# Out-projection: one burst of fp32 work per tile, with TensorE in written order

## The chip, the cores and the metric

The kernel runs on one core of a Trainium2 chip. The core has five engines that run side by side, each with its own queue in order: TensorE (PE in the profile; its weight loads are the row PEld), VectorE (DVE), ScalarE (ACT), GpSimd (POOL) and SyncE (SP, which only issues DMAs here). TensorE writes to PSUM, eight banks of 512 fp32 columns on 128 partitions; VectorE and ScalarE read PSUM. The metric is the time of one execution on the device in microseconds, as a median of several runs.

## The reference

One layer of a diffusion backbone on 256 context tokens and 2048 latent tokens, 18 tiles of 128 tokens in all. Tiles 0 and 1 are the context, 2 to 17 the latent tokens.

```python
h = rms_norm(x, g_pre) * (1 + scale) + shift
u = h @ w_in
z, xbc, dt_raw, ga, gb, gsil = split(u)
y_ssd, h_fin = ssd_branch(z, xbc, dt_raw, ..., h0)        # two scans over chunks of 128 tokens, forward and backward
    # y = y_f + y_b + d_skip * xs;  y = y * silu(z);  y = rms_norm(y, norm_g)
y_conf = conformer_branch(ga, gb, ...)                    # gate, depthwise conv, layer_norm, silu
y_conf = y_conf * silu(gsil)
out = concatenate([y_ssd, y_conf], -1) @ w_out            # 2048 -> 1024 channels
return x + gate * rms_norm(out, g_post), h_fin
```

## The kernel before

Everything up to the out-projection (input projection, convolutions, forward scan, Conformer convolution) leaves its results in DRAM. The out-projection then takes one tile of 128 tokens after the other, in `order`: 17 down to 2, then 1 and 0, since the backward scan carries its state from late tiles to early ones. `a` counts the tiles, `i` is the tile at hand, `nxt` the next one.

For each tile TensorE does 96 large matmuls (L1069, `out_part`): 16 blocks k of 128 input channels, each as three products (high x high, high x low, low x high parts, fp32r) for two halves of 512 output columns. Blocks 0 to 7 read the SSD half of the input (`yh`, `yl`), blocks 8 to 15 the Conformer half (`ph`, `pl`). The sums of a tile grow in two PSUM banks, `pso[i]`.

Between them lie smaller fp32 instructions, which prepare later tiles:

- `ssd_pre(i)`: the carried state `Sb` times C (L976, `qo`, 8 matmuls, 16 instructions in the profile), added to the stored y (L977, L978), times z (L979), squared on ScalarE (L980) and summed to `zr` (L982); then POOL carries `Sb` on (L988, L989). Its inputs ct, el, y, z and st come by DMA.
- `ssd_norm(i)`: the sum of squares over partitions, one column into bank `pm` (L995), read by VectorE (L997); then POOL raises it to the power -0.5 (L128, `yr`).
- `ssd_scale(i)`: a matmul spreads that factor into columns 128 to 255 of the same bank (L1003); VectorE multiplies y by it (L1004), and ScalarE and VectorE split the product into `yh` (L1010) and `yl` (L1011).
- `conf_pre(i)`: loads the Conformer rows `cn`, and normalizes them (L1033 to L1038). `conf_act(i)`: eight transposes (L1049, `ct`), Silu on ScalarE (L1052), times the gate (L1054). `conf_hl(i)` splits the result into `ph` (L1060) and `pl` (L1061).
- `finish(i)`: squares of the sums (L1078), factor (L1079, L1080, POOL), times gate row (L1085), plus x (L1089), store.

In the loop before, these visits of TensorE to fp32 work lie in four places: `ssd_norm(nxt)` after block 0, `ssd_pre` of the tile after `nxt` behind block 2, `ssd_scale(nxt)` behind block 5, `conf_act(nxt)` behind block 9.

PSUM banks come from two tags: "mm" with three buffers, "ss" with five. `pso` of an even tile takes two of "mm", that of an odd tile one of "mm" and one of "ss"; `pm`, `qo` and `ct` are all "ss". The weights `w_out` are loaded and split by `load_wo(k)` (DMA into `wst`, ScalarE L949 or L952, VectorE L950 or L953); k = 0 to 8 during the last input-projection matmuls (`silu_unit`, the tile `sp`), k = 9 to 15 after these, when their space comes free. The staging tile `wst` shares its buffers with `yh` and `yl`, two of each.

A planner (the Tile framework, with a simulated timeline) puts the traced instructions in order on each engine: an instruction that is ready goes first if it was traced first. It also sets the semaphores and gives out the buffers of each tag. So the order on TensorE is the planner's, and the written order its priority.

Of the kernel before, what the change touches and what calls it, by code (L numbers as in the profile page):

```python
# [8 lines left out]
F32 = mybir.dt.float32  # L9
# [4 lines left out]
MUL, ADD, SUB, MAX, MIN = ALU.mult, ALU.add, ALU.subtract, ALU.max, ALU.min  # L14
# [3 lines left out]
P = 128  # L18
D = 1024
# [3 lines left out]
NT = 18  # L23
NCTX = 2
LAT = 2048
EPS = 1e-6
# [35 lines left out]
def take(gen, n):  # L62
    for _ in range(n):
        yield next(gen, None)


@with_exitstack
def backbone_kernel(ctx, tc, xa, xt_in, cols, rows, wconv, conf_b, gp_row, bg_row, state0, w_mod, w_dt, w_in, w_out,
                    y_ctx, y_lat, new_state):
    nc = tc.nc  # L70
    V, S, G, T, DMA = nc.vector, nc.scalar, nc.gpsimd, nc.tensor, nc.sync

    const = ctx.enter_context(tc.tile_pool(name="const", bufs=1))
    psp = ctx.enter_context(tc.tile_pool(name="psum", bufs=1, space=PSUM))
# [2 lines left out]
    def bank(tag, name):  # L77
        return psp.tile([P, 512], F32, tag=tag, name=name, bufs=3 if tag == "mm" else 5)
# [32 lines left out]
    ident = const.tile([P, P], F32, name="ident")  # L111
# [5 lines left out]
    ones = const.tile([P, P], F32, name="ones")  # L117
# [8 lines left out]
    def rstd_of(pool, ms, name):  # L126
        r = pool.tile([P, 1], F32, tag="rstd", name=name, bufs=4)
        G.tensor_tensor(r, ms, nhalf, ALU.pow)  # L128
        return r
# [8 lines left out]
    def state_out(d, Ssrc, out):  # L138
        for g in range(2):
            ps = bank("ss", f"so{d}{g}")  # L140
            for c in range(4):
                T.transpose(ps[:, c * P:(c + 1) * P], Ssrc[g][:, c * P:(c + 1) * P], ident)
            so = out(f"son{d}{g}")
            S.copy(so, ps)
            DMA.dma_start(new_state[d, g * 8:(g + 1) * 8].rearrange("(c h) p n -> (h p) c n", h=2),
                          so.rearrange("p (c n) -> p c n", n=P))
# [711 lines left out]
    def run(gen):  # L858
        for _ in gen:
            pass  # L860
# [39 lines left out]
    last = [silu_unit(0, GS0, GS, j, hb, (1, 2, 0)) for j in (6, 7)]  # L900
# [23 lines left out]
    blocks = post(1, 5)  # L924
# [34 lines left out]
    def ssd_pre(i, first):  # L959
        ct = p1.tile([P, 2, P], F32, tag="ct", name=f"ct{i}", bufs=1)  # L960
        DMA.dma_start(ct, xb_slice(i, 10, 2))
        if not first:
            el = p1.tile([P, 8, P], F32, tag="el", name=f"elb{i}", bufs=1)
            decay_rows(el, i, 1)
        y = p1.tile([P, 8, P], F32, tag="y", name=f"y{i}", bufs=2)
        DMA.dma_start(y.rearrange("p q l -> p (q l)"), YP[i])
        z = p1.tile([P, 8, P], F32, tag="z", name=f"z{i}", bufs=2)
        DMA.dma_start(z, chan_slice(ZS, i))
        st = p1.tile([P, D], F32, tag="st", name=f"stl{i}", bufs=1)
        DMA.dma_start(st, ST[i])  # L970
        if not first:
            for g in range(2):
                gs = slice(4 * g, 4 * g + 4)
                po = bank("ss", f"qo{i}{g}")
                for q in range(4):
                    T.matmul(po[:, q * P:(q + 1) * P], Sb[g][:, q * P:(q + 1) * P], ct[:, g, :], start=True, stop=True)  # L976
                V.tensor_tensor(el[:, gs, :], el[:, gs, :], y8(po), MUL)  # L977
            V.tensor_tensor(y, y, el, ADD)  # L978
        V.tensor_tensor(y, y, z, MUL)  # L979
        S.activation(z, y, AF.Square)  # L980
        zr = p1.tile([P, P], F32, tag="zr", name=f"zr{i}", bufs=2)
        V.tensor_reduce(zr, z.rearrange("p q l -> p l q"), mybir.AxisListType.X, ADD)  # L982
        for g in range(2):
            sg = st[:, g * 512:(g + 1) * 512]
            if first:
                V.tensor_copy(Sb[g], sg)
            else:
                G.tensor_tensor(b3(Sb[g]), b3(Sb[g]), bh(eTb[:, i, g * 8:(g + 1) * 8]), MUL)  # L988
                G.tensor_tensor(Sb[g], Sb[g], sg, ADD)  # L989
        return y, zr  # L990

    def ssd_norm(i, yz):
        y, zr = yz
        pm = bank("ss", f"pm{i}")
        T.matmul(pm[:, 0:1], zr, ones[:, 0:1], start=True, stop=True)  # L995
        ms = p1.tile([P, 1], F32, tag="ms", name=f"yms{i}", bufs=2)
        V.tensor_scalar(ms, pm[:, 0:1], 1.0 / D, 4.0 * EPS, MUL, ADD)  # L997
        r = rstd_of(p1, ms, f"yr{i}")
        return y, r, pm

    def ssd_scale(i, yrp):
        y, r, pm = yrp
        T.matmul(pm[:, P:2 * P], r.to_broadcast([P, P]), ident, start=True, stop=True)  # L1003
        V.tensor_tensor(y, y, pm[:, P:2 * P].unsqueeze(1).to_broadcast([P, 8, P]), MUL)  # L1004
        return ssd_hl(i, y)

    def ssd_hl(i, y):
# [20 lines left out]
    def conf_pre(i):  # L1028
        n = p2.tile([P, D], F32, tag="cn", name=f"cn{i}", bufs=1)
        DMA.dma_start(n, CVC[i * P:(i + 1) * P, :] if i < 2 else CVL[(i - 2) * P:(i - 1) * P, :])  # L1030
        bs = p2.tile([P, 12], F32, tag="bs", name=f"bs{i}", bufs=2)
        for h in range(2):
            V.bn_stats(bs[:, 6 * h:6 * h + 6], n[:, h * 512:(h + 1) * 512])  # L1033
        mv = p2.tile([P, 2], F32, tag="mv", name=f"mv{i}", bufs=2)
        V.bn_aggr(mv, bs)
        V.tensor_scalar(mv[:, 1:2], mv[:, 1:2], EPS, None, ADD)
        r = rstd_of(p2, mv[:, 1:2], f"cr{i}")
        V.tensor_scalar(n, n, mv[:, 0:1], r, SUB, MUL)  # L1038
        return n

    def conf_act(i, n):
        gs = p2.tile([P, 8, P], F32, tag="gs", name=f"gsl{i}", bufs=1)
        DMA.dma_start(gs, chan_slice(GS, i))
        v = p2.tile([P, 8, P], F32, tag="v", name=f"v{i}", bufs=1)
        for g in range(2):
            ps = bank("ss", f"ct{i}{g}")
            for c in range(4):
                k = 4 * g + c
                T.transpose(ps[:, c * P:(c + 1) * P], n[:, k * P:(k + 1) * P], ident)  # L1049
            for c in range(4):  # L1050
                k = 4 * g + c
                S.activation(v[:, k, :], ps[:, c * P:(c + 1) * P], AF.Silu, bias=cv[:, C_LNB + k:C_LNB + k + 1],  # L1052
                             scale=cv[:, C_LNG + k:C_LNG + k + 1])
        V.scalar_tensor_tensor(v, v, 0.5, gs, MUL, MUL)  # L1054
        return v
# [8 lines left out]
    def out_part(pso, hl, k0, k1, ns=(0, 1)):  # L1064
        a, b = hl
        for k in range(k0, k1):
            for m, (lhs, w) in enumerate(((a, WH[k]), (a, WL[k]), (b, WH[k]))):
                for n in ns:
                    T.matmul(pso[n], lhs[:, k % 8, :], w[:, n * 512:(n + 1) * 512],  # L1069
                             start=(k == 0 and m == 0), stop=(k == 15 and m == 2))  # L1070
# [23 lines left out]
    pso = {}  # L1094
# [6 lines left out]
    run(take(blocks, 5))  # L1101
    yz = ssd_pre(i, False)
    run(take(blocks, 5))
    for k in range(6, 9):
        load_wo(k, wo2)
        run(take(blocks, 8))
    run(blocks)
    last = [silu_unit(1, GS0, GS, j, hb) for j in range(5, 8)]
    for b in range(2):
        for n, u in enumerate(last):  # L1110
            run(take(u, 8))
            if b == 0 and n == 1:
                yr = ssd_norm(i, yz)
            if b == 1 and n == 0:
                ph_b[1].close()
                p2 = ph_1.enter_context(tc.tile_pool(name="p2", bufs=1))
                yh = ssd_scale(i, yr)
                nrm = conf_pre(i)
    for u in last:
        run(u)  # L1120
# [2 lines left out]
    ph_h.close()  # L1123
    p3 = ph_1.enter_context(tc.tile_pool(name="p3", bufs=1))
    wo4 = ph_1.enter_context(tc.tile_pool(name="wo4", bufs=1, side="right"))
    for k in range(9, 16):
        load_wo(k, wo4)
    load_gg(0)
    yz = ssd_pre(order[1], False)
    for a, i in enumerate(order):  # L1130
        last = a + 1 == NT
        nxt = None if last else order[a + 1]
        pt = conf_hl(i, v)
        banks(i)
        out_part(pso[i], yh, 0, 1)
        if not last:
            yr = ssd_norm(nxt, yz)
        out_part(pso[i], yh, 1, 3)
        if a + 2 < NT:
            yz = ssd_pre(order[a + 2], order[a + 2] == NCTX - 1)  # L1140
        if not last:
            n = conf_pre(nxt)
        out_part(pso[i], yh, 3, 6)
        if not last:
            yhn = ssd_scale(nxt, yr)
        out_part(pso[i], yh, 6, 8)
        out_part(pso[i], pt, 8, 10)
        if last:
            out_part(pso[i], pt, 10, 16, (0,))
            out_part(pso[i], pt, 10, 16, (1,))  # L1150
        else:
            v = conf_act(nxt, n)
            out_part(pso[i], pt, 10, 16)
            yh = yhn
        if i == 1:
            load_gg(1)
        finish(i, pso[i], last)
    state_out(1, Sb, lambda n: p1.tile([P, D], F32, tag="z", name=n, bufs=2)[:, 0:512])
    ph_1.close()

# [58 lines left out]
```

## Time and profile before

| | |
|---|---|
| Median of 3 runs | 1888.48 us (1887.96 to 1890.22) |
| The profiled execution | 1890.22 us, its span 1888.5 us |
| Out-projection, first to last large matmul | 1426.0 to 1880.5 us |
| Mean granted TensorE clock | 0.989 |
| TensorE / VectorE / ScalarE / POOL busy in the span | 97% / 63% / 44% / 14% |

The profile is of one execution. A row of the order of time gives the start in us from the span's start, the length in us, engine, line, operation, tiles written and read, and a count where equal neighbours are merged; the end of a merged TensorE row is modelled, so the distance from one start to the next says more than the length. A row of waits gives who waited for whom, the total in us, how often, and the longest. A row of groups gives busy time in us and mean ns of one, then the idle time before.

### The profile page before, as it was taken

The numbers are of one execution on the slowest core, as the hardware profiler recorded it, in microseconds if no ns is written. First come the engines' busy times: TensorE is split into PE (matmuls) and PEld (weight loads), VectorE is DVE, ScalarE is ACT, GpSimd is POOL, SyncE is SP. The second block draws the span as 40 slices with busy tenths as digits, with TensorE's granted clock in tenths as the row PEclk, the third lists the DMA queues.
The fourth block names the chain that finished last, engine by engine and source line by source line (L and its number), as shares of the span: only waits on it lengthen the run. The fifth ranks groups of instructions, "written<-read, shape, count | busy, mean of one in ns | idle before, by whom it ended". The sixth has DMA issues, their size and how long they took to land.

```text
span 1888.5 us, 26833 instructions
## 1 busy us (share of the span) xinstructions
PE 1827.4 (97%) x9739; PEld 1500.1 (79%) x9739; DVE 1192.4 (63%) x1699; ACT 839.9 (44%) x1786; POOL 264.6 (14%) x351
## 2 busy tenths in 40 slices
PE   7899999999999999999999998999999999999998
PEld 4788887787787888888877776767787888888886
DVE  2487877776545543586596758655438767776762
ACT  3647424443455441744356666664414323222321
POOL 0002001111111100100001111100003233333220
PEclk9999999999999999999999999999999999999999
DMA  8556665564686754445587888987887565555532
GB/s 299 213 199 214 216 217 187 169 219 154 206 274 222 229 204 162 162 154 198 186 184 220 213 228 226 246 213 201 248 262 237 182 183 168 160 171 168 177 104 75
DMA packets 290400, 375.29 MB, mean 199 GB/s; under 512 B 85206, under 2 KB 187478, under 8 KB 290268
## 3 DMA queue, kind: packets, MB, share of 16 engines
q1 hardware_dynamic: 290268, 373.58, 63.9%
q8 instruction: 77, 1.26, 0.3%
q14 instruction: 55, 0.45, 0.1%
HBM read 243.92 MB, written 129.59 MB: 198 GB/s over the span
## 4 chain that ended last, share of the span: by engine, by line
PE 60%; DMA 6%; issue 4%; ACT 3%; DVE 3%; SPq 1%; POOL 1%; POOLq 0%; DVEq 0%; ACTq 0%
PE op L1069 19%; PE sp L370 6%; PE sp L371 6%; PE sp L372 6%; DMA lb<-lt 4%; PE xp L372 2%; PE xp L371 2%; PE xp L370 2%; PE ga L370 1%; PE qo L976 1%; PE ga L372 1%; PE ga L371 1%; PE py L712 1%; PE gb L370 1%; PE gb L372 1%
## 5 line engine op out<-in xcount | busy, mean ns | idle before, releaser
L676 ACT ACTIVATE lb<-lb,WB 128x128 f32<-128x128 f32 x576 | 184.2, 391 | 150.9 <-POOL lb L668 149.0
L370 PE MATMUL sp<-hh,wh 128*128 128x512 f32 (+1 forms) x640 | 239.3, 374 | 1.9 <-DVE sth L542 1.9
L371 PE MATMUL sp<-hl,wh 128*128 128x512 f32 (+1 forms) x640 | 237.6, 371 | 0.0
L372 PE MATMUL sp<-hh,wl 128*128 128x512 f32 (+1 forms) x640 | 237.0, 370 | 0.0
L668 POOL TENSOR_SCALAR_AFFINE_SELECT lb<-lb 128x512 f32<-128x512 f32 x144 | 108.7, 759 | 751.8 <-ACT el L665 393.8
L370 PE MATMUL xp<-hh,wh 128*128 128x512 f32 (+1 forms) x480 | 178.0, 372 | 5.3 <-ACT wh L345 3.4
L371 PE MATMUL xp<-hl,wh 128*128 128x512 f32 (+1 forms) x480 | 178.2, 372 | 0.2 <-DVE hl L291 0.2
L372 PE MATMUL xp<-hh,wl 128*128 128x512 f32 (+1 forms) x480 | 178.1, 371 | 0.0
L467 DVE SCALAR_TENSOR_TENSOR cva<-raw,cwh,cva 128x1280 f32<-128x1280 f32 (+1 forms) x96 | 142.5, 1493 | 15.3 <-ACT cva L461 13.4
L370 PEld LDWEIGHTS sp<-hh,wh 128*128 128x128 f32 x640 | 121.1, 189 | 23.9 <-DVE sth L542 2.3
L372 PEld LDWEIGHTS sp<-hh,wl 128*128 128x128 f32 x640 | 121.1, 189 | 20.7 <-issue 0.2
L371 PEld LDWEIGHTS sp<-hl,wh 128*128 128x128 f32 x640 | 121.1, 189 | 20.3 <-issue 0.5
L370 PE MATMUL gb<-hh,wh 128*128 128x512 f32 (+1 forms) x320 | 121.5, 380 | 6.1 <-DVE gth L531 6.1
L370 PE MATMUL ga<-hh,wh 128*128 128x512 f32 (+1 forms) x320 | 120.2, 376 | 3.2 <-ACT gth L528 3.2
L371 PE MATMUL gb<-hl,wh 128*128 128x512 f32 (+1 forms) x320 | 119.4, 373 | 0.0
L372 PE MATMUL gb<-hh,wl 128*128 128x512 f32 (+1 forms) x320 | 119.3, 373 | 0.0
L372 PE MATMUL ga<-hh,wl 128*128 128x512 f32 (+1 forms) x320 | 118.3, 370 | 0.0
L371 PE MATMUL ga<-hl,wh 128*128 128x512 f32 (+1 forms) x320 | 118.2, 369 | 0.0
L582 DVE SCALAR_TENSOR_TENSOR cg<-cg,cv 128x256 f32<-128x256 f32 x240 | 112.3, 495 | 2.5
L542 DVE SCALAR_TENSOR_TENSOR sth<-sth,sp 128x512 f32<-128x512 f32 (+1 forms) x80 | 50.4, 630 | 96.0 <-ACT sth L541 96.0
L370 PEld LDWEIGHTS xp<-hh,wh 128*128 128x128 f32 x480 | 91.3, 190 | 22.0 <-ACT wh L345 4.1
L680 DVE TENSOR_TENSOR lb<-lb,lb 128x512 f32<-128x512 f32 x72 | 50.2, 697 | 88.6 <-ACT lb L676 55.8
(219 smaller groups left out, 3862.9 us busy)
## 6 DMA issues: line engine op xcount, KB each, us to landing
lb<-lt SPq DMA_DIRECT2D x144, 256.0 KB, 4.6
wr<-in_w_in SPq DMA_DIRECT2D x88, 256.0 KB, 4.9
whd<-wh SPq DMA_DIRECT2D x44, 512.0 KB, 3.2
wld<-wl SPq DMA_DIRECT2D x44, 512.0 KB, 4.6
wh<-whd SPq DMA_DIRECT2D x44, 512.0 KB, 5.7
wl<-wld SPq DMA_DIRECT2D x44, 512.0 KB, 5.6
xT<-xb SPq DMA_DIRECT2D x18, 512.0 KB, 5.6
yp<-yg SPq DMA_DIRECT2D x36, 256.0 KB, 4.8
```

The source lines that it names most:

```text
L370: T.matmul(ps[:, :BN], wh[:, k, :], hh[:, k, :], start=(k == 0), stop=False)
L371: T.matmul(ps[:, :BN], wh[:, k, :], hl[:, k, :], start=False, stop=False)
L372: T.matmul(ps[:, :BN], wl[:, k, :], hh[:, k, :], start=False, stop=(k == KT - 1))
L467: V.scalar_tensor_tensor(a[:, :n], raw[:, t:t + n], cwh[:, ct * 5 + t:ct * 5 + t + 1], a[:, :n], MUL, ADD)
L542: V.scalar_tensor_tensor(th, th, 1.0, ps[:, :BN], ADD, MUL)
L582: V.scalar_tensor_tensor(acc, g[:, t:t + 256], cv[:, w0 + t:w0 + t + 1], acc, MUL, ADD)
L668: G.affine_select(E[g, hq, d], E[g, hq, d], pattern=[[0, 4], [sg, P]], compare_op=ALU.is_ge, fill=NEG, base=0, channel_multiplier=-sg)
L676: S.activation(lb[:, h, :], lb[:, h, :], AF.Exp, bias=WB[:, i, c + h:c + h + 1])
L680: V.tensor_tensor(a, a, E[g, hq, 1], ADD)
L712: T.matmul(py[g][j * HD:(j + 1) * HD, q * P:(q + 1) * P], xt[g][:, h * HD:(h + 1) * HD], E[g, hq, 0][:, t, :], start=True, stop=True)
L976: T.matmul(po[:, q * P:(q + 1) * P], Sb[g][:, q * P:(q + 1) * P], ct[:, g, :], start=True, stop=True)
L1069: T.matmul(pso[n], lhs[:, k % 8, :], w[:, n * 512:(n + 1) * 512], start=(k == 0 and m == 0), stop=(k == 15 and m == 2))
```

## The change

The visits to fp32 work are moved together, into one burst behind block 3 of each tile, and they serve three different tiles:

- spreading (`ssd_scale`) for the next tile, then the sum of squares (`ssd_norm`) for the tile after it, both in one bank `pm` that is taken in the burst;
- the eight transposes (`conf_act`) for the next tile;
- the carried state (`ssd_pre`) for the third tile on.

`ssd_pre` thus runs one tile further ahead: y gets a third buffer, `ssd_pre(order[1])` moves into the last input-projection matmuls, and `conf_pre(order[1])`, `ssd_norm(order[1])` and `ssd_pre(order[2])` come before the loop. `load_wo(8)` moves behind the input projection, to k = 9 to 15. A wrapper `InOrder` around TensorE ties each of its instructions in the loop behind the one traced before, so that there TensorE runs in written order. The other engines stay with the planner.

```diff
+class InOrder:
+    def __init__(self, tc, eng):
+        self.tc, self.eng, self.on = tc, eng, False
+    def _put(self, ins):
+        return self.tc.keep_in_program_order(ins) if self.on else ins
+    def matmul(self, *a, **k):
+        return self._put(self.eng.matmul(*a, **k))
+    def transpose(self, *a, **k):
+        return self._put(self.eng.transpose(*a, **k))
...
-    V, S, G, T, DMA = nc.vector, nc.scalar, nc.gpsimd, nc.tensor, nc.sync
+    V, S, G, T, DMA = nc.vector, nc.scalar, nc.gpsimd, InOrder(tc, nc.tensor), nc.sync
...
-        y = p1.tile([P, 8, P], F32, tag="y", name=f"y{i}", bufs=2)
+        y = p1.tile([P, 8, P], F32, tag="y", name=f"y{i}", bufs=3)
...
-    def ssd_norm(i, yz):
+    def ssd_norm(i, yz, ps):
         y, zr = yz
-        pm = bank("ss", f"pm{i}")
-        T.matmul(pm[:, 0:1], zr, ones[:, 0:1], start=True, stop=True)
+        T.matmul(ps[:, 0:1], zr, ones[:, 0:1], start=True, stop=True)
         ms = p1.tile([P, 1], F32, tag="ms", name=f"yms{i}", bufs=2)
-        V.tensor_scalar(ms, pm[:, 0:1], 1.0 / D, 4.0 * EPS, MUL, ADD)
-        r = rstd_of(p1, ms, f"yr{i}")
-        return y, r, pm
-    def ssd_scale(i, yrp):
-        y, r, pm = yrp
-        T.matmul(pm[:, P:2 * P], r.to_broadcast([P, P]), ident, start=True, stop=True)
-        V.tensor_tensor(y, y, pm[:, P:2 * P].unsqueeze(1).to_broadcast([P, 8, P]), MUL)
+        V.tensor_scalar(ms, ps[:, 0:1], 1.0 / D, 4.0 * EPS, MUL, ADD)
+        return y, rstd_of(p1, ms, f"yr{i}")
+    def ssd_scale(i, yr, ps):
+        y, r = yr
+        T.matmul(ps[:, P:2 * P], r.to_broadcast([P, P]), ident, start=True, stop=True)
+        V.tensor_tensor(y, y, ps[:, P:2 * P].unsqueeze(1).to_broadcast([P, 8, P]), MUL)
...
-    for k in range(6, 9):
+    for k in range(6, 8):
         load_wo(k, wo2)
-        run(take(blocks, 8))
+        run(take(blocks, 12))
...
             if b == 0 and n == 1:
-                yr = ssd_norm(i, yz)
+                yr = ssd_norm(i, yz, bank("ss", f"pm{i}"))
+                yz = ssd_pre(order[1], False)
...
-                yh = ssd_scale(i, yr)
+                yh = ssd_scale(i, yr, bank("ss", f"pr_{i}"))
...
-    for k in range(9, 16):
+    for k in range(8, 16):
         load_wo(k, wo4)
     load_gg(0)
-    yz = ssd_pre(order[1], False)
+    n = conf_pre(order[1])
+    yr = ssd_norm(order[1], yz, bank("ss", f"pm{order[1]}"))
+    yz = ssd_pre(order[2], False)
+    T.on = True
     for a, i in enumerate(order):
         last = a + 1 == NT
         nxt = None if last else order[a + 1]
         pt = conf_hl(i, v)
         banks(i)
-        out_part(pso[i], yh, 0, 1)
+        out_part(pso[i], yh, 0, 4)
+        yhn = None
         if not last:
-            yr = ssd_norm(nxt, yz)
-        out_part(pso[i], yh, 1, 3)
+            pm = bank("ss", f"pm{i}_")
+            yhn = ssd_scale(nxt, yr, pm)
+            if a + 2 < NT:
+                yr = ssd_norm(order[a + 2], yz, pm)
+            v = conf_act(nxt, n)
+        if a + 3 < NT:
+            yz = ssd_pre(order[a + 3], order[a + 3] == NCTX - 1)
         if a + 2 < NT:
-            yz = ssd_pre(order[a + 2], order[a + 2] == NCTX - 1)
-        if not last:
-            n = conf_pre(nxt)
-        out_part(pso[i], yh, 3, 6)
-        if not last:
-            yhn = ssd_scale(nxt, yr)
-        out_part(pso[i], yh, 6, 8)
-        out_part(pso[i], pt, 8, 10)
-        if last:
+            n = conf_pre(order[a + 2])
+        out_part(pso[i], yh, 4, 8)
+        yh = yhn
+        if not last:
+            out_part(pso[i], pt, 8, 16)
+        else:
+            out_part(pso[i], pt, 8, 10)
             out_part(pso[i], pt, 10, 16, (0,))
             out_part(pso[i], pt, 10, 16, (1,))
-        else:
-            v = conf_act(nxt, n)
-            out_part(pso[i], pt, 10, 16)
-            yh = yhn
         if i == 1:
             load_gg(1)
         finish(i, pso[i], last)
+    T.on = False
```

## The prediction

> **What bounds the kernel now.** I read the page first (busy time by engine), then the stretches, the waits of TensorE in the out-projection, and its instructions in order of time.
>
> ```profile
> span 1888.5 us, 26833 instructions
> PE 1827.4 (97%) x9739; PEld 1500.1 (79%) x9739; DVE 1192.4 (63%) x1699; ACT 839.9 (44%) x1786; POOL 264.6 (14%) x351
> ```
>
> TensorE is busy for 97% of the span. The stretches (busy time of PE, PEld, DVE, ACT, POOL, then granted clock, DMA share, GB/s) show how this is in the out-projection:
>
> ```profile
> 1446.00:1450.00 4.00, 2.06 (x8) 1.04 (x6) 4.00 (x3) 3.43 (x7) 2.06 (x1) 1.00 0.75 218
> 1450.00:1457.00 7.00, 5.53 (x17) 4.42 (x18) 7.00 (x7) 3.63 (x7) 0.00 (x0) 0.76 0.58 178
> 1583.40:1608.70 25.30, 25.30 (x125) 21.05 (x124) 17.63 (x21) 7.20 (x16) 8.10 (x7) 1.00 0.56 171
> ```
>
> A middle tile has TensorE busy for 25.30 of 25.30 us; VectorE has 7.7 us free in it. Only the first tile has gaps, and the waits of TensorE from 1425 to 1870 us are two, both for weights of that tile:
>
> ```profile
> PE op L1069 <- DVE wol L953: 2.2, 1, 2.2
> PE op L1069 <- ACT woh L952: 1.2, 1, 1.2
> ```
>
> So each microsecond that TensorE loses or saves in a middle tile moves the end, and nothing else does. TensorE in order of time (start, us, what): starts of tiles 1, 2 and 3, a middle tile with its four visits to fp32 work, and the last tile, which has none.
>
> ```profile
> 1424.27 1.95 PE L976 MATMUL qo<-ct,Sb 128*128 128x128 f32 x16
> 1425.97 0.71 PE L1069 MATMUL op<-woh,yh 128*128 128x512 f32 x2
> ...
> 1456.78 0.63 PE L1069 MATMUL op<-woh,yh 128*128 128x512 f32 x2
> ...
> 1482.11 0.63 PE L1069 MATMUL op<-woh,yh 128*128 128x512 f32 x2
> ...
> 1584.77 0.28 PE L995 MATMUL pm<-ones,zr 128*128 128x1 f32 x2
> ...
> 1587.74 1.95 PE L976 MATMUL qo<-ct,Sb 128*128 128x128 f32 x16
> 1589.44 0.71 PE L1069 MATMUL op<-woh,yh 128*128 128x512 f32 x2
> ...
> 1593.62 0.38 PE L1003 MATMUL pm<-ident,yr 128*128 128x128 f32 x2
> 1593.75 0.72 PE L1069 MATMUL op<-woh,yh 128*128 128x512 f32 x2
> ...
> 1599.43 1.03 PE L1049 MATMUL ct<-ident,cn 128*128 128x128 f32 x8
> ...
> 1858.30 0.63 PE L1069 MATMUL op<-woh,yh 128*128 128x512 f32 x2
> ...
> 1863.77 0.62 PE L1069 MATMUL op<-woh,yh 128*128 128x512 f32 x2
> ...
> 1880.48 1.03 PE L142 MATMUL so<-ident,Sb 128*128 128x128 f32 x8
> ```
>
> A tile takes 1482.11-1456.78 = 25.33 us; the first takes 1456.78-1425.97 = 30.81, so 5.48 are lost in it. The order is already the written one, visit by visit.
>
> **The change part by part.**
>
> *One visit in place of four.* The last tile needs 1880.48-1858.30 = 22.18 us for its 96 large matmuls, so the four visits cost 25.33-22.18 = 3.15 us. They hold 28 fp32 instructions; at the 1.70/16 = 0.106 us of the qo group (1587.74 to 1589.44) these alone are 2.97. Changing over is thus worth at most 0.18 us a tile for all four, and merging saves 0 to 0.18. I take 0: 0.18 is a ceiling that leaves nothing for the one changeover that stays. Over 16 tiles the bound is 2.9 us.
>
> *Spreading and sum of squares in one bank.* This decides. In the new burst `ssd_scale(nxt)` writes columns 128 to 255 of bank `pm` (L1003), VectorE multiplies y by them (L1004), and then `ssd_norm` of the tile after writes column 0 of the same bank (L995). The columns differ and no data passes. Does the second write wait for VectorE's read? The trace of before has no such pair with TensorE, but one like it in the scan: ACT reads columns 0 to 255 of `pb` (L774), VectorE reads the same columns (L775), and ACT then copies columns 256 to 511 (L776), with no data from L775. The waits of ACT (total, times, longest):
>
> ```profile
> ACT cb L776 <- DVE btl L775: 12.5, 5, 4.0
> ```
>
> ACT stood 12.5 us for a read of other columns in its bank. If two reads of a bank are kept apart, a write and a read are too. So L995 waits for L1004, and since TensorE now keeps written order, the eight transposes, the 16 carried-state matmuls and the rest of the tile stand behind it.
>
> [...]
>
> The price: the burst starts when 24 large matmuls of the tile are through, 1863.77-1858.30 = 5.47 us after its start. L1003 takes 0.38 there, then L1004, whose mean is
>
> ```profile
> L1004 DVE TENSOR_TENSOR y<-y,pm 128x1024 f32<-128x1024 f32 x17 | 20.6, 1209 | 2.9 <-PE pm L1003 2.9
> ```
>
> and from VectorE's end to TensorE's next weight load a handover costs 0.05 (1450.21+1.21 = 1451.42 to 1451.47):
>
> ```profile
> 1450.21 1.21 DVE L953 TENSOR_TENSOR wol<-wst,woh 128x1024 fp32r<-128x1024 f32 x1
> 1451.47 0.50 PEld L1069 LDWEIGHTS op<-wol,ph 128*128 128x128 f32 x2 [2.64 <-DVE wol L953]
> ```
>
> With 0.05 each way L995 starts 0.38+0.05+1.21+0.05 = 1.69 after L1003, where the next matmul now starts 0.13 after it (1593.62 to 1593.75): 1.55 us lost, if VectorE is free. Is it? Around the tile start at 1608.70 it does the end of the tile before:
>
> ```profile
> 1608.44 1.05 ACT L1060 CAST ph<-v 128x1024 fp32r<-128x1024 f32 x1 [5.41 <-PE op L1069]
> ...
> 1610.45 0.20 ACT L1078 ACTIVATION_READ_ACCUMULATOR o<-op 128x1 f32 x1
> ...
> 1610.30 0.81 DVE L1038 TENSOR_SCALAR cn<-cn,mv,cr 128x1024 f32<-128x1024 f32 x1 [0.66 <-POOL cr L128]
> 1611.02 1.22 DVE L1061 TENSOR_TENSOR pl<-v,ph 128x1024 fp32r<-128x1024 f32 x1
> ...
> 1612.23 0.15 DVE L1079 TENSOR_TENSOR oms<-oms 128x1 f32<-128x1 f32 x1
> ...
> 1612.90 0.55 POOL L128 TENSOR_TENSOR or<-oms,nhalf 128x1 f32<-128x1 f32 x1
> 1613.49 1.41 DVE L1085 SCALAR_TENSOR_TENSOR o<-op,or,gg 128x512 f32<-128x512 f32 x2 [0.92 <-POOL or L128]
> 1614.93 1.45 DVE L1089 TENSOR_TENSOR o<-o,xr 128x1024 f32<-128x1024 f32 x1
> ```
>
> Today it is free at 1616.38, 7.68 after the start. In the new order cn is normalized in the middle of the tile and POOL's other power goes into the burst, so the chain runs from the squares' end (1610.65, 1.95 after the start): 0.30 for oms, 0.55 POOL, 1.41, 1.45, and 0.15 for handovers, free at about 5.8, just before L1004 can start at 5.90. As it stands today L1004 would end at 8.89, and 3.35 would be lost. I take 1.55, since what delays VectorE today is moved away. TensorE has no slack, so this adds in full: 15 tiles (all with a tile two places on, the first apart) x 1.55 = 23.3 us.
>
> *First tile.* State and `conf_pre` of tile 2 move ahead, and 1.8 us of qo work and 0.14 of L995 go in front of tile 1, which starts at about 1428.0, its burst at 1433.5. There L995 needs zr of tile 3. Today the same chain ends so:
>
> ```profile
> 1435.48 2.00 DVE L982 TENSOR_REDUCE zr<-z 128x128 f32<-128x1024 f32 x1
> ```
>
> 1437.48 is 13.2 after its qo group (1424.27). The new one is issued at about 1426.2, so zr comes at 1439.4, 5.8 us too late, plus up to 1.2 for L1004 in the same queue. These take the place of the 5.48 lost today, since weights have longer to arrive. Row two of the stretches shows a granted clock of 0.76 right after a half-idle stretch; a gap of 6 us would bring that again, 0.24 of 7 us, or 1.7. Net +2.5 taken; bounds -5.5 (nothing lost) and +8 (weights late as well: k=8 is now also loaded here, and two staging buffers hold yh and yl until k=7).
>
> *The rest.* A third y buffer lets y load a tile earlier, hidden as now. The burst needs five "ss" banks where an odd tile leaves four; pm comes free 0.2 us after L995, while the fifth is wanted 1.9 us after it (0.14, 0.79 transposes, 0.85 half of qo): nothing. Moved state DMAs and POOL's updates have a tile's time before use. Conf transposes move earlier; v is needed 17 us later.
>
> Sum: 23.3 + 2.5 + 0 = +25.8. The profiled execution took 1890.22 (span 1888.5); the median of the runs, 1888.48, lies 1.7 under that time and on the span, so I add to 1888.5: 1914.3.
>
> **The rivals.**
>
> - *Bank not guarded between columns.* L995 goes straight through; only the first tile's +2.5 and up to -2.9 from merging remain: 1888 to 1891. Against it stands the wait of ACT above.
> - *Faster.* The first tile's loss goes: zr in time at 1433.5, that is 7.3 us after its qo group instead of 13.2, weights in time too. Without the guard that gives 1888.5-5.5 = 1883.0; with it, nothing under 1903. It decides only if no wait falls on L995.
> - *VectorE late.* The chain at the tile start stays as it is today: 15 x 3.35 = 50.3, with +2.5, 1941. Against it: the work that delays it is traced elsewhere. Half-idle stretches would then recur, and a lower clock with them. [...]
>
> **How the numbers follow.** Main case 0.76, VectorE late 0.10, no guard 0.09, faster 0.05. The main case's own range: low 1888.5+23.3-5.5-2.9 = 1903, high 1888.5+23.3+8+4 (0.25 more a tile) = 1924. For 8 in 10 it reaches up to the third rival: 1903 to 1942. A change of under 0.2% (3.8 us) can't be told from none. Slower 0.86, within 0.09, faster 0.05.
>
> **What would show it.** A wait of TensorE's L995 (or its weight load) for VectorE's y of L1004, some 1.5 us, in each tile, 23 us or so in total; a period near 26.9 us; the visits as one block. Wrong would be: no such wait and a period of 25.3, or a wait for transposes' cn, zr or a bank instead, or gaps above 3 us with the clock below 1.

## The result and the profile after

The changed kernel is slower: 1918.79 us median of 4 runs (1915.38 to 1921.08) against 1888.72 (1887.96 to 1890.22), ratio 1.0157 with a 95% interval of 1.0137 to 1.0176. The prediction said 1914.3 in a range of 1903 to 1942. In the changed file the lines of the prediction stand 14 to 16 further down (L1004 is L1018, L982 is L998, L953 is L969), and all matmuls of TensorE carry the wrapper's lines, L77 and L80, so they are told apart by their tiles: `pm<-ident` is the spread (L995 and L1003 of before are `pm<-ones` and `pm<-ident`).

The page of after, span and engines:

```profile
span 1919.0 us, 26840 instructions
PE 1838.5 (96%) x9739; PEld 1507.2 (79%) x9739; DVE 1183.4 (62%) x1699; ACT 840.1 (44%) x1786; POOL 267.1 (14%) x351
```

TensorE ran the same 9739 matmuls. Its busy time grew by 11 us, the span by 30.5: most of the loss is idle time. What ended it, from the waits of TensorE in the out-projection of after (total, times, longest):

```profile
PE pm__13216 L77 <- DVE zr L998: 7.8, 1, 7.8
PE pm__13795 L77 <- DVE y L1018: 1.3, 1, 1.3
...
PE pm__16093 L77 <- DVE y L1018: 1.3, 1, 1.3
```

Fifteen tiles wait for VectorE's y, each 1.3 us, and the first burst waits 7.8 for zr. Of the waits for weights, the only ones before, 1.3 of 3.4 us are left, 0.8 and 0.5. A middle tile and then the first tile of after, in stretches (busy time of PE, PEld, DVE, ACT, POOL; granted clock, DMA share, GB/s):

```profile
1573.44:1600.30 26.86, 25.55 (x125) 21.13 (x124) 17.20 (x20) 7.23 (x16) 8.16 (x7) 1.00 0.57 162
1427.98:1465.99 38.01, 28.96 (x127) 23.88 (x126) 30.76 (x34) 17.64 (x28) 12.19 (x11) 0.87 0.87 255
```

The middle tile takes 26.86 in place of 25.32, at full clock, with the same work; the first takes 38.01 in place of 30.81. TensorE in order of time, in the first burst and a middle one of after:

```profile
1433.55 0.38 PE L77 MATMUL pm__13216<-ident,yr 128*128 128x128 f32 x2
1441.69 0.59 PE L77 MATMUL pm__13216<-ones,zr 128*128 128x1 f32 x2 [7.76 <-DVE zr L998]
...
1462.31 0.62 PE L77 MATMUL op<-woh,pl 128*128 128x512 f32 x2
1463.70 0.73 PE L77 MATMUL op<-woh,ph 128*128 128x512 f32 x2 [0.77 <-ACT woh L968]
1464.95 0.73 PE L77 MATMUL op<-wol,ph 128*128 128x512 f32 x2 [0.53 <-DVE wol L969]
...
1552.05 0.38 PE L77 MATMUL pm__13988<-ident,yr 128*128 128x128 f32 x2
1553.74 0.38 PE L77 MATMUL pm__13988<-ones,zr 128*128 128x1 f32 x2 [1.31 <-DVE y L1018]
1553.99 1.07 PE L80 MATMUL ct<-ident,cn 128*128 128x128 f32 x8
1554.89 1.95 PE L77 MATMUL qo<-ct,Sb 128*128 128x128 f32 x16
```

The burst is one block. Its sum of squares starts 1553.74-1552.05 = 1.69 us after the spread, where 0.13 would do: 1.56 lost. In between VectorE does this:

```profile
1551.05 1.23 DVE L1103 TENSOR_TENSOR o<-o,xr 128x1024 f32<-128x1024 f32 x1
1552.47 1.22 DVE L1018 TENSOR_TENSOR y<-y,pm__13988 128x1024 f32<-128x1024 f32 x1 [0.19 <-PE pm__13988 L77]
```

L1018 starts when the spread is through and ends at 1553.69; 0.05 later TensorE goes on.

The account, from the starts of the tiles: tile 1 starts 2.01 us later (1427.98 against 1425.97, work moved ahead of it), takes 7.20 longer, and from tile 2 to the start of the last tile 422.74 us pass in place of 401.52, 21.22 more. The rest is equal (0.02): 30.45, the difference of the spans. By cause: 15 x 1.56 = 23.4 is the stall; the moved 2.0 are saved again at the other end; about 7 are left, all in the first tile.

### The profile page after: what moved, and what is told of

It is laid out like the page before. It is cut to its first block, busy times and chain, and to the rows that moved or that the text cites. A ratio compares the mean times of both kernels' runs of the same rounds, so it can differ in the third digit from the quotient of the medians.

```text
span 1919.0 us, 26840 instructions
## 1 busy us (share of the span) xinstructions
PE 1838.5 (96%) x9739; PEld 1507.2 (79%) x9739; DVE 1183.4 (62%) x1699; ACT 840.1 (44%) x1786; POOL 267.1 (14%) x351
## 4 chain that ended last, share of the span: by engine, by line
PE 78%; DMA 8%; DVE 5%; ACT 4%; issue 3%; SPq 1%; POOL 1%; POOLq 0%; DVEq 0%; ACTq 0%
PE sp L77 20%; PE op L77 19%; PE xp L77 13%; PE ga L77 7%; PE gb L77 7%; DMA lb<-lt 3%; PE pst L77 2%; PE py L77 2%; PE po L77 2%; ACT lb L692 1%; PE qo L77 1%; PE cp L77 1%; DMA wr<-in_w_in 1%; DVE y L1018 1%; DMA wm<-in_w_mod 1%
## 5 line engine op out<-in xcount | busy, mean ns | idle before, releaser
L77 PE MATMUL sp<-hh,wh 128*128 128x512 f32 (+1 forms) x640 | 239.9, 375 | 2.5 <-DVE sth L558 2.5
L77 PE MATMUL sp<-hl,wh 128*128 128x512 f32 (+1 forms) x640 | 238.1, 372 | 0.0
L77 PE MATMUL sp<-hh,wl 128*128 128x512 f32 (+1 forms) x640 | 237.8, 372 | 0.0
L684 POOL TENSOR_SCALAR_AFFINE_SELECT lb<-lb 128x512 f32<-128x512 f32 x144 | 113.5, 793 | 743.2 <-ACT el L681 410.8
L77 PE MATMUL xp<-hh,wh 128*128 128x512 f32 (+1 forms) x480 | 179.2, 375 | 6.5 <-ACT wh L361 4.4
L77 PE MATMUL xp<-hl,wh 128*128 128x512 f32 (+1 forms) x480 | 179.2, 374 | 0.0
L77 PE MATMUL xp<-hh,wl 128*128 128x512 f32 (+1 forms) x480 | 179.1, 373 | 0.0
L77 PEld LDWEIGHTS sp<-hh,wh 128*128 128x128 f32 x640 | 121.5, 190 | 24.7 <-DVE sth L558 3.0
L77 PEld LDWEIGHTS sp<-hh,wl 128*128 128x128 f32 x640 | 121.5, 190 | 20.8 <-issue 0.2
L77 PEld LDWEIGHTS sp<-hl,wh 128*128 128x128 f32 x640 | 121.5, 190 | 20.6 <-issue 0.5
L77 PE MATMUL gb<-hh,wh 128*128 128x512 f32 (+1 forms) x320 | 121.6, 380 | 2.7 <-DVE gth L547 2.7
L77 PE MATMUL ga<-hh,wh 128*128 128x512 f32 (+1 forms) x320 | 120.2, 376 | 1.7 <-ACT gth L544 1.7
L77 PE MATMUL gb<-hh,wl 128*128 128x512 f32 (+1 forms) x320 | 119.5, 374 | 0.0
L77 PE MATMUL gb<-hl,wh 128*128 128x512 f32 (+1 forms) x320 | 119.4, 373 | 0.0
L77 PE MATMUL ga<-hh,wl 128*128 128x512 f32 (+1 forms) x320 | 118.2, 369 | 0.0
L77 PE MATMUL ga<-hl,wh 128*128 128x512 f32 (+1 forms) x320 | 118.2, 369 | 0.0
L77 PEld LDWEIGHTS xp<-hh,wh 128*128 128x128 f32 x480 | 92.0, 192 | 23.7 <-ACT wh L361 5.0
```

What stands on the lines that cost most here:

```text
L77: return self._put(self.eng.matmul(*a, **k))
L684: G.affine_select(E[g, hq, d], E[g, hq, d], pattern=[[0, 4], [sg, P]], compare_op=ALU.is_ge, fill=NEG, base=0, channel_multiplier=-sg)
```

## Experiments

Beside these runs the kernel before took 1883.7 to 1886.4 us (medians), not 1888.7, so times are compared by ratio, and the steady tiles by their period, from one tile's start to the next, which repeats within 0.04 us in one run (odd and even tiles apart). What a tile loses is counted from 25.31, the period of the burst without any wait (the second run below).

**The sum of squares in a bank of its own.**

```diff
-                yr = ssd_norm(order[a + 2], yz, pm)
+                yr = ssd_norm(order[a + 2], yz, bank("ss", f"pn{i}_"))
```

> The sum of squares gets a bank of its own; order and pinning stay as in the changed kernel. Theory (one bank holds the spread that VectorE reads and the column that TensorE writes next): the 15 waits of L995's successor for VectorE's y, 1.5 us each, are gone and the period falls from 26.87 to 25.3 in even tiles. In odd tiles, where the output holds one of the five small banks, the burst wants six banks of four: the first carried-state matmul comes 1.15 us after the spread, its bank is free 1.64 after it, so about 0.5 us a tile is lost there. Time 1919 - 23.4 + 4 = about 1899.5; the first tile's 7.8 us for zr stays. Rival (the wait is for VectorE's queue or for y itself, not for the bank): period stays 26.87, time 1919.

Two neighbouring tiles of it in stretches (columns as above), and TensorE in the odd one:

```profile
1511.43:1536.71 25.28, 25.28 (x125) 21.06 (x124) 18.17 (x20) 7.10 (x16) 8.15 (x7) 1.00 0.55 172
1536.71:1562.53 25.82, 25.51 (x126) 21.09 (x125) 18.17 (x20) 7.12 (x16) 8.15 (x7) 1.00 0.55 168
```

```profile
1542.19 0.38 PE L77 MATMUL pm__13992<-ident,yr 128*128 128x128 f32 x2
1542.41 0.28 PE L77 MATMUL pn__13999<-ones,zr 128*128 128x1 f32 x2
...
1543.93 2.02 PE L77 MATMUL qo<-ct,Sb 128*128 128x128 f32 x16 [0.31 <-issue]
```

The sum of squares follows the spread at once. The 0.5 us come back in odd tiles, at the carried state, which wants a sixth bank: it starts at 1543.93, 0.10 after VectorE's multiply has left the spread's bank (1543.83). The trace names no releaser there, so that it is this bank is argued from these times and from the even tiles, which have one bank more and do not wait. One timed execution: 1894.76 beside 1886.4 of before. The wait was the bank's: written order, VectorE's work and y are the same as in after.

**Sum of squares first, in its own bank.**

```diff
-            yhn = ssd_scale(nxt, yr, pm)
-            if a + 2 < NT:
-                yr = ssd_norm(order[a + 2], yz, pm)
+            yrn = ssd_norm(order[a + 2], yz, bank("ss", f"pn{i}_")) if a + 2 < NT else None
+            yhn = ssd_scale(nxt, yr, bank("ss", f"pm{i}_"))
+            yr = yrn
```

> Sum of squares first and in a bank of its own, then the spread in another. Theory: its bank is free again 0.5 us after the burst starts and serves the carried state in odd tiles, so no tile waits: period 25.3, time 1919 - 23.4 = about 1895.5, with the first tile's loss (about 7 us more than before) left. Rival (a pinned burst costs by itself, also without the shared bank): above 1900.

```profile
1562.15:1587.46 25.31, 25.31 (x125) 21.10 (x124) 18.25 (x20) 7.11 (x16) 8.15 (x7) 1.00 0.55 172
```

That stretch is one of its tiles: from tile 3 on there is no idle time at all, in even and odd tiles. Ratio 1.0034 (1.0021 to 1.0048), or 6.4 us more than before where 7 were expected. What is lost lies in two tiles, not one: tile 1 takes 37.45, and tile 2, which begins behind two waits for weights (1.73 and 0.53), takes 26.84, 1.53 over the period, for which no row here shows the reason. A merged, pinned burst is worth 25.32-25.31 = 0.01 us a tile against four visits.

**Same bank, three ways to read it for a shorter time.** Order changed, so that the wait is for the read of one column:

```diff
+            yrn = ssd_norm(order[a + 2], yz, pm) if a + 2 < NT else None
             yhn = ssd_scale(nxt, yr, pm)
-            if a + 2 < NT:
-                yr = ssd_norm(order[a + 2], yz, pm)
+            yr = yrn
```

> Same bank, but the sum of squares goes before the spread in the burst. Theory: now the spread waits for VectorE's read of one column (0.16 us) instead of its multiply of 1.22, some 0.45 us a tile with the handovers and what VectorE still has to finish, period about 25.75, time about 1919 - 15 x 1.1 = 1902. Rival (the pinned order of the burst itself costs the time): period stays near 26.87.

The sum of squares behind the transposes (`v = conf_act(nxt, n)` moves up between the two calls):

> Same bank, sum of squares behind the eight transposes, which take 0.93 us and do not use this bank. Theory: the wait shrinks by just that, from 1.55 to about 0.6 us a tile, period 25.95, time 1919 - 15 x 0.93 = about 1905. Rival (the wait is a fixed price of a pinned change of bank, or VectorE is late anyway): the wait stays near 1.5.

The spread copied out by VectorE before the multiply:

```diff
-        V.tensor_tensor(y, y, ps[:, P:2 * P].unsqueeze(1).to_broadcast([P, 8, P]), MUL)
+        pc = p1.tile([P, P], F32, tag="zr", name=f"pc{i}", bufs=3)
+        V.tensor_copy(pc, ps[:, P:2 * P])
+        V.tensor_tensor(y, y, pc.unsqueeze(1).to_broadcast([P, 8, P]), MUL)
```

> Same bank and same order, but VectorE copies the 128 spread columns out first (estimate 0.3 us, from 0.16 for one column and 0.69 for 512) and multiplies y from the copy. Theory: what counts is how long the bank is being read: the wait falls to 0.38 + 0.3 + 0.1 - 0.13 = about 0.65 us a tile, period 26.0, time about 1905, although VectorE works 0.3 us more in each tile. Rival (TensorE waits for y or for VectorE's queue): the wait grows to about 1.8 us, time about 1923.

TensorE in a middle tile of these three, in this order:

```profile
1569.48 0.28 PE L77 MATMUL pm__14181<-ones,zr 128*128 128x1 f32 x2
1570.10 0.46 PE L77 MATMUL pm__14181<-ident,yr 128*128 128x128 f32 x2 [0.34 <-DVE yms L1012]
```

```profile
1574.54 0.38 PE L77 MATMUL pm__14181<-ident,yr 128*128 128x128 f32 x2
...
1576.24 0.38 PE L77 MATMUL pm__14181<-ones,zr 128*128 128x1 f32 x2 [0.44 <-DVE y L1018]
```

```profile
1569.58 0.38 PE L77 MATMUL pm__14193<-ident,yr 128*128 128x128 f32 x2
1570.35 0.38 PE L77 MATMUL pm__14193<-ones,zr 128*128 128x1 f32 x2 [0.38 <-DVE pc L1019]
```

VectorE in the third, between them (the multiply, from the copy, follows):

```profile
1570.00 0.29 DVE L1019 COPY pc<-pm__14193 128x128 f32<-128x128 f32 x1 [0.18 <-PE pm__14193 L77]
```

| kernel | what is read under the guard | period | lost per tile | expected period | one time |
|---|---|---|---|---|---|
| after | 1.22 us | 26.87 | 1.56 | | 1918.79 (median) |
| same bank, sum first | 0.16 us | 25.80 | 0.49 | 25.75 | 1903.32 |
| same bank, behind transposes | 1.22, less 0.87 of transposes | 26.03 | 0.72 | 25.95 | 1906.86 |
| spread copied out | 0.29 us | 25.93 | 0.62 | 26.0 | 1900.84 |

The loss follows the time for which the bank is read, less what TensorE has to do in other banks meanwhile. In the third VectorE works more and y is no earlier, and still the tile is 0.94 shorter: TensorE waits for the bank, not for y.

One tile of the first of the three took 28.0 us, where the next of its kind (without carried state) takes 24.03. VectorE came 2.4 us late there:

```profile
1778.84 0.46 PE L77 MATMUL pm__15725<-ident,yr 128*128 128x128 f32 x2 [2.69 <-DVE yms L1012]
1779.13 1.82 PE L80 MATMUL ct<-ident,cn 128*128 128x128 f32 x8
```

```profile
1770.39:1798.40 28.01, 25.32 (x110) 20.80 (x108) 12.40 (x17) 7.26 (x16) 1.65 (x3) 0.94 0.34 113
```

Behind this gap of 2.7 us the clock was lower: the eight transposes take 1.82 in place of 1.04, and the granted clock over the tile is 0.94. This is the rival "VectorE late" in one tile. In after VectorE is free at 1552.28, 0.19 before its multiply can start: so near did that rival lie.

**Order left to the planner.**

```diff
-    T.on = True
+    T.on = False
```

> The changed kernel with one bank, but TensorE not held to written order: the planner may put other matmuls ahead of the sum of squares. Theory: the bank guard stays, but large matmuls fill the wait, so no wait for y is seen; period 25.3 to 25.5, time 1890 to 1898 with what is left of the first tile. Rival (the bank alone costs the time, whatever the order): 1915 to 1919.

TensorE's fp32 work in a middle tile, where the large matmuls are left out:

```profile
1560.47 0.38 PE L77 MATMUL pm__14181<-ident,yr 128*128 128x128 f32 x2
...
1561.56 1.95 PE L77 MATMUL qo<-ct,Sb 128*128 128x128 f32 x16
...
1565.20 0.28 PE L77 MATMUL pm__14181<-ones,zr 128*128 128x1 f32 x2
```

The planner puts the sum of squares of the same bank 4.7 us after the spread, and nothing waits. Period 25.34 on average, ratio 1.0000 (0.9987 to 1.0012), better than the 1890 to 1898 expected. So it takes two things for the loss: one bank, and an order that lets nothing pass.

Most of the first tile's loss goes with the pinned order as well. Here are tiles 1 and 2 of this kernel, whose work is interleaved, as one stretch; then VectorE's sum to zr and TensorE's two instructions around it:

```profile
1421.42:1478.97 57.55, 53.95 (x252) 44.59 (x251) 47.75 (x54) 24.65 (x43) 22.18 (x18) 0.94 0.77 237
```

```profile
1433.67 1.89 DVE L998 TENSOR_REDUCE zr<-z 128x128 f32<-128x1024 f32 x1
```

```profile
1419.63 2.03 PE L77 MATMUL qo<-ct,Sb 128*128 128x128 f32 x16
...
1441.80 0.42 PE L77 MATMUL pm__13216<-ones,zr 128*128 128x1 f32 x2
```

The two tiles take 57.55 us, against 64.86 in after and 56.14 in before. Yet zr comes no earlier, 1435.56-1419.63 = 15.9 us after its qo group (15.4 in after). TensorE does other work until then, and its one wait there is 3.6 us, for `ph`.

**The first tile.** Six experiments on the 7 us that are left, with TensorE in written order again.

```diff
-        out_part(pso[i], yh, 0, 4)
+        out_part(pso[i], yh, 0, 4 if a else 8)
...
-        out_part(pso[i], yh, 4, 8)
+        if a:
+            out_part(pso[i], yh, 4, 8)
```

> Only the first tile is changed: its burst goes behind k = 8 instead of 4, 5.4 us later. Theory (first tile lost 8.0 us for zr and 3.0 at half clock behind that gap): zr comes at about 1441.6 and the burst at 1439, so 2 to 3 us of wait stay, no half clock, and 5 to 8 us are gained: 1911 to 1914. Rival (weights that land late bound this tile in any case): the gain turns into waits for wol and woh, time 1916 to 1919.

A miss: the time falls into the rival's range, but weights are not the reason. The longest wait of TensorE in its first tile, and VectorE ahead of it:

```profile
PE pm__13240 L77 <- DVE y L1018: 6.2, 1, 6.2
```

```profile
1437.54 1.23 DVE L969 TENSOR_TENSOR wol<-wst,woh 128x1024 fp32r<-128x1024 f32 x1 [1.66 <-ACT woh L968]
...
1439.82 1.21 DVE L1018 TENSOR_TENSOR y<-y,pm__13240 128x1024 f32<-128x1024 f32 x1
```

zr is in time, but the multiply of y stands behind a weight split that waits for its cast, and the shared bank makes that TensorE's wait. Tiles 1 and 2 take 66.9 together, against 64.9 in after. Ratio 1.0173 (1.0153 to 1.0192), not told apart from after's.

Both repairs at once (own bank and sum first, first burst behind k = 8):

> Both repairs: sum of squares first in its own bank, and the first tile's burst behind k = 8. Theory: the gains add, 1895.5 - 5 to 8 = 1887 to 1891, no better than the kernel before, since merging the visits is worth 0.01 us a tile. Rival (merging is worth the bound of 0.18 us a tile, or the pinned order saves something else): 1883 to 1886.

```profile
PE op L77 <- DVE wol L969: 2.5, 3, 1.8
PE pn__13240 L77 <- DVE zr L998: 1.3, 1, 1.3
```

Now the moved burst helps: zr is waited for 1.3 us, tile 1 takes 33.61 (37.45 with sum first and own bank alone) and every other one with carried state 25.31. Ratio 1.0022 (1.0005 to 1.0040), 1 to 8 us above before where -1.5 to +2.5 were expected; the two ranges overlap.

The first tile as before, with four visits, the burst from the second tile on:

> Every middle tile has the pinned burst with the sum of squares first in its own bank; the first tile keeps the kernel before's four visits, its loading of k = 8 and two y buffers, and the run three tiles ahead starts only at its end. Theory (the merged burst is worth nothing, and what the own-bank kernel still lost, 6 us, is the first tile's lead): within 0.1% of the kernel before, ratio 0.999 to 1.001, period 25.31. Rival (the burst also costs in the prologue or at the end): ratio 1.002 or more. Rival (four visits cost their bound of 0.18 us a tile): ratio 0.9985.

Ratio 1.0020 (1.0002 to 1.0039): its middle is the rival's, but the interval reaches down into the theory's range, so the time alone does not decide. The trace shows a cost at the start: the period is 25.30, but tile 1 takes 36.34 although its four visits stand as before. Of the 5.53 more, 1.92 are the sum of squares and the carried state of later tiles, added at its end (1449.74 to 1451.66), and most of the rest is a new wait:

```profile
PE op L77 <- DVE pl L1075: 3.3, 1, 3.3
```

The planner had placed VectorE's work anew: `pl` starts only at 1439.28, behind a weight split and the multiply of y.

Then three edits to bring zr earlier, all on the changed kernel. `conf_pre(order[1])` behind `ssd_pre(order[2])`:

> The changed kernel with one line moved: the normalization of tile 2's convolution rows (its transfer and its statistics on VectorE) stands behind the carried state of tile 3 instead of ahead of it. Theory (zr is late because VectorE's queue waits 1.9 us for those rows and then does their statistics first): zr comes 2 to 3 us earlier after the qo group and the wait of 7.8 falls to about 5. Rival (VectorE simply has too much to do in that stretch, or the rows are then late for the transposes): the first tile stays within 1 us of 38.0.

The wait stayed (7.6), and so did VectorE's order: the planner put the statistics ahead of the state again. The edit did not reach what it was to test. Tile 1 took 39.67, one execution 1920.22 beside 1884.54 of before.

```diff
-            V.tensor_tensor(wl, wr, wh.bitcast(F32), SUB)
+            (G if k < 12 else V).tensor_tensor(wl, wr, wh.bitcast(F32), SUB)
```

> The changed kernel with the low halves of four weight blocks (k = 8 to 11) subtracted on POOL instead of VectorE. Theory (the weight splits of 1.22 us stand in front of zr in VectorE's queue): two of them are gone ahead of zr, which comes 2 to 2.5 us earlier; the wait of 7.8 falls to about 5.5 and the time by 2 to 3 us. Rival (zr waits for transfers, not for VectorE's time): the wait stays 7 to 8, and the low halves come later (POOL takes about 2.1 us each), so the first tile grows.

The wait grew to 9.7, which neither side expected, and tile 1 to 41.36, as the rival said; one execution took 1916.26. POOL and VectorE of this kernel in that stretch:

```profile
1425.89 5.86 POOL L969 TENSOR_TENSOR wol<-wst,woh 128x1024 fp32r<-128x1024 f32 x2 [1.74 <-ACT woh L968]
```

```profile
1426.30 3.24 DVE L995 TENSOR_TENSOR y<-y,z 128x1024 f32<-128x1024 f32 x1
...
1429.53 3.31 DVE L1068 SCALAR_TENSOR_TENSOR v<-v,gsl 128x1024 f32<-128x1024 f32 x1
```

While POOL subtracts, two operations of VectorE take 3.24 and 3.31 us, where after has 1.22 for each. What was taken off VectorE's queue came back as slower work in it.

State of tile 3 ahead of the statistics, VectorE held to that order:

> The changed kernel, but ahead of the first tile VectorE is held to an order in which the carried state of tile 3 and its zr come before the statistics of tile 2's convolution rows and before one weight split. Both theories: zr comes some 4.8 us earlier (no wait of 1.9 for the rows, 1.3 of statistics and 1.2 of the spread's multiply behind it), so the wait of 7.8 falls to about 3. Theory 1 (the order on VectorE made the first tile long): the tile falls from 38.0 to 33 to 35 us. Theory 2 (the burst wants zr and the normalized rows cn, and VectorE's work for both, some 13 us, does not fit between the qo group and the burst in any order): cn is late in place of zr, the transposes wait 4 to 6 us for it, and the tile stays within 1.5 us of 38.0.

```profile
PE pm__13216 L77 <- DVE y L1020: 10.3, 1, 10.3
PE ct L80 <- DVE cn L1054: 4.1, 1, 4.1
```

```profile
1433.64 1.23 DVE L969 TENSOR_TENSOR wol<-wst,woh 128x1024 fp32r<-128x1024 f32 x1 [3.01 <-ACT woh L968]
1436.62 1.23 DVE L1070 SCALAR_TENSOR_TENSOR v<-v,gsl 128x1024 f32<-128x1024 f32 x1 [1.75 <-DMA gsl<-gs]
```

Neither theory had the size: tile 1 took 47.6, one execution 1927.81 beside 1883.71 of before. A weight split and v moved ahead of zr, and VectorE stood 3.01 and 1.75 us in front of them for a cast and a transfer. Late cn showed as theory 2 said, but behind a longer wait.

No version beats the kernel before.

## Why the prediction was right

- *TensorE is the bound, four visits cost nothing* (0 taken, up to 0.18 a tile): measured 0.01 a tile, the burst pinned and its sum in a bank of its own.
- *One bank makes the sum of squares wait for VectorE's multiply* (1.55 a tile, 23.3 in all; period near 26.9): measured 1.56, 23.4 and 26.87. The chain of it held as well: VectorE free 5.71 us after the tile's start (5.8 predicted), the multiply at 5.90, handovers of 0.04 to 0.05. The own-bank run shows the cause, the three shorter reads its size. That a write and a read are kept apart as two reads are was the author's inference from ACT's wait of 12.5 us; in after TensorE's write waits for VectorE's read of other columns of its bank, at 1.56 us a tile. What the chip would do without the guard was not tried. Nor can these runs tell a guard by bank from a guard by tile, since `bank` gives out a whole bank as one tile.
- *First tile +2.5 (bounds -5.5 and +8)*: this term was mis-sized. About +7 was measured, which accounts for the 4.5 us by which the forecast fell short; it lies within the bounds, but of the terms behind it three were too small. The sum was 5.8 of wait and up to 1.2 for the multiply, plus 1.7 at a lower clock, less 5.48, with nothing for weights: 2.0 to 3.2. The wait came to 8.0 (8.14 from the spread to the sum of squares, less 0.13). zr came 1441.63-1426.20 = 15.4 us after the start of its qo group, not 13.2: it is the last of a queue of VectorE work with the rows' statistics, two weight splits, v and the multiply, and VectorE stood 1.9 us for the rows:

```profile
1430.87 1.29 DVE L1047 BATCH_NORM_STATS2 bs<-cn 128x6 f32<-128x512 f32 x2 [1.91 <-DMA cn<-cvl]
...
1437.87 1.22 DVE L1018 TENSOR_TENSOR y<-y,pm__13216 128x1024 f32<-128x1024 f32 x1
...
1439.72 1.91 DVE L998 TENSOR_REDUCE zr<-z 128x128 f32<-128x1024 f32 x1
```

The half clock at the gap cost more, too, than the 1.7 us taken for it:

```profile
1437.40:1447.60 10.20, 5.91 (x27) 5.91 (x28) 9.15 (x10) 5.94 (x11) 2.13 (x3) 0.50 1.05 333
```

TensorE worked 5.91 us at a clock of 0.50 and so lost 3.0. With 8.0 at the burst and 1.8 for weights, which the prediction put at nothing (the rows from 1462.31 reach to 1465.53, where three times 0.47 would do), the first tile loses 12.8 in place of 5.5: 7.3 by this sum, 7.20 measured. Which single work on VectorE makes zr late stays open: bringing it forward failed in three ways, and VectorE's order was the planner's or ran into loads. Shown is what makes a late zr cost time. With TensorE's order left to the planner zr was as late, and tiles 1 and 2 together were 7.3 us shorter, 1.5 of them the stall of tile 2; and a later burst, once the bank is not shared, takes 3.8 us off tile 1.
- *The rest at 0*: five banks in the burst did suffice in after. The margin is small, as the own-bank run shows, where a sixth costs 0.5 in odd tiles.
- *The rivals*: no guard between columns is refuted for this program. VectorE late did not come in the steady tiles, by 0.19 us. Faster came in no run. The clock of 0.76 in before stood behind waits of 1.22 and 2.20 us with work between them; in after the stall of 1.56 us a tile left the granted clock at 1.00, from 1447.63 to 1915.20.

## What to carry to other kernels

With TensorE held to written order, two results in one PSUM bank were one resource here: a read of 1.22 us cost 1.56 a tile, one of 0.16 cost 0.49. So count for how long the bank is read, and give the next writer another bank (no idle time from tile 3 on with the sum first), or put other work between them (0.72 lost a tile with the transposes there). Where the order was the planner's, the same sharing, with zr as late, cost nothing here (ratio 1.0000), so a bank plan has to be looked at again whenever an order is pinned. And the first round of a loop that runs further ahead needs an account of its own, engine by engine in queue order: its work is the same, its time to do it is not.

## What was not expected of the hardware

- VectorE beside POOL: with two weight splits on POOL, two operations of VectorE took 3.24 and 3.31 us beside POOL's subtraction, 2.7 times the 1.22 that after has for each without it; POOL's two took 5.86 us there, and one of them 2.36 at 1439.46, where VectorE stood idle for most of it.
- The half clock: in before the granted clock was 0.50 for 3.41 us (1451.34 to 1454.75), behind gaps of 1.22 and 2.20 us with work between them, neither of them as long as the half clock itself. In after it was 0.50 for 10.24 us (1437.39 to 1447.63), from a time when the gap of 7.8 still lasted. With the same bank and the sum first it was 0.94 over the one tile with a gap of 2.7. The gaps of 1.3 us once a tile in after did not bring it: the granted clock is 1.00 from 1447.63 to 1915.20.
